# State-space input tables made from transposed factors on GpSimd, and the in-chunk kernel made from the output tables

## The chip, the cores and the metric

The kernel runs on one core of a Trainium2 chip. Its engines work side by side, each through its own list of instructions in order: TensorE (PE: matrix products and transposes), VectorE (DVE), ScalarE (ACT) and GpSimd (POOL). SyncE (SP) issues the transfers between DRAM and the on-chip memory, which 16 DMA engines carry out; its list too is worked off in order, and a transfer that has to wait for something holds up those behind it. The metric is the device time of one execution in microseconds (us), as the median of several runs.

## The reference, cut to what matters

The program is a two-layer encoder trunk on 1024 frames of 1024 channels. Its first layer has two branches, and the change concerns one of them, a diagonal complex state-space layer ("S5") over 64 groups of 16 channels with 64 states each, worked in chunks of 64 frames:

```python
lb_re = mag * jnp.cos(aim * dt);  lb_im = mag * jnp.sin(aim * dt)      # one pole per state
bb_re = coef_re[..., None] * bre - coef_im[..., None] * bim            # input matrix, group x state x 16
bb_im = coef_re[..., None] * bim + coef_im[..., None] * bre
...
bu_re = jnp.einsum('tbgh,gnh->tbgn', u_c, bb_re)                       # input of every state
bu_im = jnp.einsum('tbgh,gnh->tbgn', u_c, bb_im)
pr, pim, zr, zi = lax.associative_scan(_complex_affine_combine, (a_r, a_i, bu_re, bu_im), axis=0)
xr = zr + pr * s_re - pim * s_im                                       # states, with the carry
y = (jnp.einsum('tbgn,ghn->tbgh', xr, cre) - jnp.einsum('tbgn,ghn->tbgh', xi, cim) + dsk * u_c)
```

After it come a GELU and a gated linear unit. The second branch (retention) and the second layer (a convolution module) are untouched.

## The kernel before, in words

The state-space layer is not worked frame by frame. Frames are taken in strips of eight. Within a strip the output is a small triangular (Toeplitz) matrix applied to the eight frames, the in-chunk kernel; across strips the states are carried by a scan over 128 strips. The 64 groups are 32 pairs of groups, whose two times 64 states fill the 128 partitions, and the pairs go in eight blocks B of four.

Three pairs of tables are made per block, by `s5_tables` on GpSimd, each from small factors by `outer` (L785 to L792): for both the real and the imaginary part two products and one sum or difference, so six operations over 128x512 elements for a pair of tables and 18 for a block. All 18, of all blocks, are chained in the order in which they are written:

- Mr, Mi, the input tables: powers of the pole (`pr`, `pi`, step j = 0 to 7) times the input matrix (`bbr`, `bbi`), states on the partitions. The factors are read repeated (one along the 16 channels, the other along the eight steps).
- Tc, Ts, rotation factors for the scan.
- W3, the output tables: powers of the pole (steps 1 to 8) times the output matrix C (`cr`, `nci`).

`s5_states` (L830 to L897) then loads U, the block's input in strips, transposes M on TensorE into W2 (L837, eight transposes per block, each pair of banks copied by ScalarE at L839), multiplies W2 with U into v (L848), rotates and scans v on VectorE (L856 to L876) into the states S, and makes the in-chunk kernel `kp` from M and a block-diagonal copy of C (`cbr`, `cbni`, loaded; L882 and L883, eight products). The kernel is copied (Kg, L885), gets the direct term d on its first 16 columns (L886), is transposed on TensorE (kt, L888), copied (Kt, L890), stored to DRAM (L892, 64 KB), read back with overlapping rows as the Toeplitz matrix Wd (L895), and reordered into W1 (L897). `s5_out` (L912, L918) makes the output y of a block from W1, U, W3 and S, one block later.

All this runs beside a long sequence of ordinary products: `mm_u` (the input projection, eight column blocks `u_block`) and then `mm_g` (the gates, 16 column blocks, two to a state-space block). Each is a 1024-deep product in three passes (L276 to L278: high parts, low times high, high times low) on tiles of 128x512, 24 of them for half a column block. Below, "product n" counts these passes on TensorE from the start of the program. The weights for them, `wf_g`, are loaded by SP, cast by ScalarE (L267), and reduced to the low part by VectorE or GpSimd (L268). Other transfers in the same queue are the input sums (`xa`, `xt`) and weight sums (`a`, `ws`, `va`, `vs`) for later stages.

What order the instructions get on each engine is decided when the program is built, by a scheduler with a model of times; each engine then follows its list. Tables have buffers of their own: M and W2 one set, T and W3 two.

## Time and profile before

| | |
|---|---|
| runs | 1179.49, 1176.93, 1178.66 us; median 1178.66 |
| profiled execution: first to last instruction | 1173.9 us |
| median above that span | 4.8 us |
| granted clock of TensorE | 0.999 |
| TensorE busy | 1161.3 us, 99% |
| VectorE, ScalarE, GpSimd busy | 910.5, 545.1, 713.5 us |
| DMA, over the span | 270.66 MB, 231 GB/s |

The profile is of one execution; the span runs from its first to its last instruction, and the run's own time has the start and the end of the program besides. PE's busy time overlaps itself, as products are pipelined: one that is shown with 0.39 us starts about 0.23 us behind the one before it. A row of the timeline gives start, duration, engine, line, operation, tiles and count; a row of a group gives busy time and mean ns, and behind the second bar the idle time of the engine before it with what ended it; a row of the table of stretches gives the busy time of each engine with its instructions, the clock, the share of the DMA engines that was busy, and what they moved.

### The profile page before, as it was taken

To read this page: it belongs to the slowest core of one execution; us is meant where nothing else is said; L and a number is where in the kernel's file an instruction comes from. 1 tells how busy PE (TensorE), PEld (TensorE's weight loads), DVE (VectorE), ACT (ScalarE), POOL (GpSimd) and SP (SyncE) were. 2 spreads that over 40 slices of the span, in tenths; PEclk is the share of its full clock that TensorE was granted. 3 is DMA by queue.
4 is the path that set the end of the run, shared out by engine and by line. 5 is a ranking of instruction groups with operands and counts; after the bars stand their busy time and mean duration, and the time that the engine had idled before them with its cause. 6 is when DMAs were issued, how large, how long until landed. Compare 5 with 4: busy or idle time off the path is not lost.

```text
span 1173.9 us, 17492 instructions
## 1 busy us (share of the span) xinstructions
PE 1161.3 (99%) x6150; PEld 965.5 (82%) x6150; DVE 910.5 (78%) x1507; ACT 545.1 (46%) x821; POOL 713.5 (61%) x507
## 2 busy tenths in 40 slices
PE   9999999999999999999999999999999999999997
PEld 7888888888888888887788888888888888888887
DVE  7875789999717475689777888479999999999643
ACT  7212343332226642123645544367756678544662
POOL 2049999888843245664444034348894689977742
PEclk9999999999999999999999999999999999999999
DMA  9353378778789765765988468965448553357863
GB/s 344 109 178 109 134 270 312 272 269 282 273 307 325 268 228 192 251 190 180 362 313 304 160 220 268 309 232 188 161 158 306 216 182 132 134 176 243 281 247 138
DMA packets 131192, 270.66 MB, mean 231 GB/s; under 512 B 12832, under 2 KB 41760, under 8 KB 130976
## 3 DMA queue, kind: packets, MB, share of 16 engines
q1 hardware_dynamic: 129952, 265.35, 66.5%
q10 hardware_dynamic: 1152, 4.19, 0.9%
q8 instruction: 48, 0.79, 0.3%
q14 instruction: 40, 0.33, 0.1%
HBM read 193.54 MB, written 71.76 MB: 226 GB/s over the span
## 4 chain that ended last, share of the span: by engine, by line
PE 91%; DMA 4%; DVE 2%; SPq 1%; ACT 1%; POOL 1%; issue 1%; DVEq 0%; POOLq 0%; ACTq 0%
PE mm_g L277 8%; PE mm_g L278 8%; PE mm_g L276 7%; PE mm_w L278 4%; PE mm_w L277 4%; PE mm_w L276 4%; PE mm_a L278 2%; PE mm_b L277 2%; PE mm_a L276 2%; PE mm_b L278 2%; PE mm_a L277 2%; PE mm_b L276 2%; PE mm_u L278 2%; PE mm_oc L278 2%; PE mm_u L277 2%; PE mm_oc L277 2%
## 5 line engine op out<-in xcount | busy, mean ns | idle before, releaser
L1461 DVE SCALAR_TENSOR_TENSOR cv<-u,convw,cv 128x512 f32<-128x512 f32 x358 | 244.7, 750 | 5.0 <-ACT cv L1447 3.5
L1441 POOL TENSOR_TENSOR tp<-tp,tp 128x512 f32<-128x512 f32 x104 | 138.9, 1338 | 28.7 <-ACT tp L1440 23.4
L278 PE MATMUL mm_g<-xh,wl_g 128*128 128x512 f32 x256 | 100.8, 394 | 0.0
L277 PE MATMUL mm_g<-xl,wh_g 128*128 128x512 f32 x256 | 100.7, 394 | 0.0
L276 PE MATMUL mm_g<-xh,wh_g 128*128 128x512 f32 x256 | 100.5, 393 | 0.0
L1440 ACT ACTIVATE tp<-u,convw 128x512 f32<-128x512 f32 x104 | 69.6, 713 | 9.6 <-POOL tp L1441 9.4
L277 PEld LDWEIGHTS mm_g<-xl,wh_g 128*128 128x128 f32 x256 | 48.1, 188 | 11.2 <-issue 1.6
L278 PEld LDWEIGHTS mm_g<-xh,wl_g 128*128 128x128 f32 x256 | 48.0, 188 | 10.5
L276 PEld LDWEIGHTS mm_g<-xh,wh_g 128*128 128x128 f32 x256 | 48.1, 188 | 9.6
L278 PE MATMUL mm_oc<-zh,wl_woc 128*128 128x512 f32 (+1 forms) x152 | 54.5, 360 | 0.2 <-DMA wl_woc<-lo_woc 0.2
L276 PE MATMUL mm_oc<-zh,wh_woc 128*128 128x512 f32 (+1 forms) x152 | 54.3, 362 | 0.0
L277 PE MATMUL mm_oc<-zl,wh_woc 128*128 128x512 f32 (+1 forms) x152 | 54.0, 357 | 0.0
L276 PE MATMUL mm_glu<-yh,wh_glu 128*128 128x512 f32 x128 | 50.0, 392 | 1.3 <-ACT sg L1250 1.3
L277 PE MATMUL mm_u<-xl,wh_u 128*128 128x512 f32 x128 | 50.1, 391 | 1.0 <-DVE xl L390 0.9
L276 PE MATMUL mm_g<-h1h,wh_cg 128*128 128x512 f32 x128 | 50.3, 393 | 0.0
L276 PE MATMUL mm_a<-h1h,wh_ca 128*128 128x512 f32 x128 | 50.3, 393 | 0.0
L278 PE MATMUL mm_b<-h1h,wl_cb 128*128 128x512 f32 x128 | 50.3, 393 | 0.0
L232 ACT CAST lh<-lf 128x512 fp32r<-128x512 f32 x32 | 19.5, 618 | 65.9 <-DMA lf<-w_c 59.3
L278 PE MATMUL mm_a<-h1h,wl_ca 128*128 128x512 f32 x128 | 50.0, 391 | 0.0
L277 PE MATMUL mm_glu<-yl,wh_glu 128*128 128x512 f32 x128 | 50.0, 392 | 0.0
L278 PE MATMUL mm_g<-h1h,wl_cg 128*128 128x512 f32 x128 | 49.9, 390 | 0.0
L277 PE MATMUL mm_g<-h1l,wh_cg 128*128 128x512 f32 x128 | 49.9, 390 | 0.0
(811 smaller groups left out, 3637.3 us busy)
## 6 DMA issues: line engine op xcount, KB each, us to landing
wf_g<-w_ab SPq DMA_DIRECT2D x16, 512.0 KB, 5.4
a<-w_out SPq DMA_DIRECT2D x32, 256.0 KB, 4.4
ws<-a SPq DMA_DIRECT2D x32, 256.0 KB, 4.8
lf<-w_c SPq DMA_DIRECT2D x32, 256.0 KB, 5.3
wf_p<-ws SPq DMA_DIRECT2D x16, 512.0 KB, 4.1
wf_cb<-w_c SPq DMA_DIRECT2D x16, 512.0 KB, 4.9
wf_ca<-w_c SPq DMA_DIRECT2D x16, 512.0 KB, 4.7
wl_cb<-lo_cb SPq DMA_DIRECT2D x16, 512.0 KB, 3.4
```

The lines of the kernel that those rows point to most:

```text
L232: self.nc.scalar.copy(hi[:], f[:])
L276: nc.tensor.matmul(ps, wh[:, kb, :], xh, start=start, stop=False)
L277: nc.tensor.matmul(ps, wh[:, kb, :], xl, start=False, stop=False)
L278: self.last_mm = nc.tensor.matmul(ps, wl[:, kb, :], xh, start=False, stop=stop)
L1440: nc.scalar.mul(sk[:], u[:, k:k + HALF], cw[:, nb, k:k + 1])
L1441: gp.tensor_tensor(s0[:], s0[:], sk[:], op=ALU.add)
L1461: v.scalar_tensor_tensor(dst[:], *tap, accs_[i][:], op0=ALU.mult, op1=ALU.add)
```

## The change

The M tables and their transposes are gone. The transposed tables W2 are made directly:

- `s5_turned`, once, early in the sequence `mm_u`: TensorE transposes the powers of the pole (`pr`, `pi`, four transposes) and the input matrix (`bbr`, `bbi`, eight); ScalarE copies the results, and four stores put them into DRAM (`ptr`, `pti`, 128 KB each; `btr`, `bti`, 256 KB each).
- For this `bbr` and `bbi` are laid out with the channel ahead of the pair, and GpSimd writes them with a stride.
- Per block four loads of 256 KB read these back repeated: PTr, PTi have every step's row 16 times (once for each channel), BTr, BTi have the 16 channels' rows eight times. GpSimd multiplies them into W2 by `outer`, six operations over 128x512 elements with nothing repeated in the operands. The order in a block is now T, W2, W3. PT, BT and W2 have one buffer each, so the loads of a block wait for the W2 of the block before.
- W3 gets 16 columns more ahead of its 128, filled by ScalarE with C itself (two copies per block). The in-chunk kernel is the product of a block-diagonal copy of the input matrix (`bblk`, made once: two fills by GpSimd, four copies by ScalarE) and the first 128 of these columns. It comes out transposed as needed, so the transpose kt and its copy are gone; but its rows are then written to DRAM by eight stores per block, with runs of 16 elements (64 bytes) in DRAM, in place of one store with rows of 512 bytes.
- `cbr`, `cbi` (two loads of 512 KB at the start) and the negation of one of them are gone. The pool of the early tiles closes after the sixth `u_block` in place of the fourth.

```diff
+                if (nb, h) == (6, 0):
+                    with tc.issue_after(self.last_mm.ins):
+                        self.s5_turned(ev)
...
-        self.cbr, self.cbni = load("s5_cbr", (NP, 32)), load("s5_cbi", (NP, 32))
+        self.bblk = [sp.tile([P, NP, 32], F32, name=f"s5_bblk{c}") for c in "ri"]
+        for b in self.bblk:
+            nc.gpsimd.memset(b[:], 0.0)
...
-        tt(self.bbr[:], x1[0], x1[1], ALU.subtract, gp)
-        tt(self.bbi[:], x1[2], x1[3], ALU.add, gp)
+        tt(self.bbr[:].rearrange("p h q -> p q h"), x1[0], x1[1], ALU.subtract, gp)
+        tt(self.bbi[:].rearrange("p h q -> p q h"), x1[2], x1[3], ALU.add, gp)
+    def s5_turned(self, tp):
+        nc = self.nc
+        self.pt_d = [self.dram.tile([8, 32, P], F32, name=f"pt{c}") for c in "ri"]
+        self.bt_d = [self.dram.tile([16, 32, P], F32, name=f"bt{c}") for c in "ri"]
+        def turn(name, srcs, dsts):
+            ps = self.bank(f"turn_{name}")
+            for i, src in enumerate(srcs):
+                nc.tensor.transpose(ps[:, i * P:(i + 1) * P], src, self.ident[:])
+            t = tp.tile([P, 8, P], F32, name=f"turned_{name}", tag="xin", bufs=8)[:, :4, :]
+            nc.scalar.copy(t.rearrange("p i n -> p (i n)"), ps[:])
+            n = len(srcs) // len(dsts)
+            for i, dst in enumerate(dsts):
+                nc.sync.dma_start(dst.rearrange("(i p) n -> p i n", p=P), t[:, i * n:(i + 1) * n, :])
...
+        for blk, b in zip(self.bblk, (self.bbr, self.bbi)):
+            for g in range(2):
+                r = slice(64 * g, 64 * g + 64)
+                nc.scalar.copy(blk[r, :, 16 * g:16 * g + 16], b[r].rearrange("p h q -> p q h"))
...
-        Mr, Mi = self.big(f"Mr_{B}", "Mr", 1), self.big(f"Mi_{B}", "Mi", 1)
-        made = [self.outer(B, Mr[:], Mi[:], bj(self.bbr), bj(self.bbi), pj(self.pr), pj(self.pi), vm)]
...
+        made = [self.outer(B, Tc[:], Ts[:], ea(self.e2[0]), ea(self.e2[1]), eb(self.e1[0]), eb(self.e1[1]), vt)]
+        PT, BT = ([self.big(f"{n}{c}_{B}", n + c, 1) for c in "ri"] for n in ("PT", "BT"))
+        for t, d in zip(PT, self.pt_d):
+            nc.sync.dma_start(t[:], bass.AP(tensor=d.tensor, offset=d.offset + qs.start * P,
+                                            ap=[[32 * P, 8], [0, 16], [1, 4 * P]]))
+        for t, d in zip(BT, self.bt_d):
+            nc.sync.dma_start(t[:], bass.AP(tensor=d.tensor, offset=d.offset + qs.start * P,
+                                            ap=[[0, 8], [32 * P, 16], [1, 4 * P]]))
+        W2 = [self.big(f"W2{c}_{B}", f"W2{c}", 1) for c in "ri"]
+        made.append(self.outer(B, W2[0][:], W2[1][:], BT[0][:], BT[1][:], PT[0][:], PT[1][:], lambda ap: ap))
+        W3 = w.tile([P, 2, 4, 9 * 16], F32, name=f"W3_{B}", tag="W3", bufs=2)
+        for c, t in enumerate((self.cr, self.nci)):
+            nc.scalar.copy(W3[:, c, :, 0:16], t[:, qs, :])
+        made.append(self.outer(B, W3[:, 0, :, 16:], W3[:, 1, :, 16:], pj(self.pr), pj(self.pi), bj(self.cr),
+                               bj(self.nci), vm, ALU.add, ALU.subtract))
...
-        for nm, M in (("r", Mr), ("i", Mi)):
-            ps = self.bank(f"w2{nm}_{B}")
-            for q in range(4):
-                nc.tensor.transpose(ps[:, q * P:(q + 1) * P], M[:, q, :], self.ident[:])
-            t = self.big(f"W2{nm}_{B}", f"W2{nm}", 1)
-            nc.scalar.copy(t[:].rearrange("p q n -> p (q n)"), ps[:])
...
-        for q in range(4):
-            o = kp[q * 32:(q + 1) * 32, :P]
-            nc.tensor.matmul(o, self.cbr[:, q0 + q, :], Mr[:, q, :], start=True, stop=False)
-            nc.tensor.matmul(o, self.cbni[:, q0 + q, :], Mi[:, q, :], start=False, stop=True)
+        for c in range(2):
+            made += [nc.tensor.matmul(kp[q * 32:(q + 1) * 32, :P], self.bblk[c][:, q0 + q, :], W3[:, c, q, :P],
+                                      start=c == 0, stop=c == 1) for q in range(4)]
...
-        nc.tensor.transpose(kp[:, :P], Kg[:], self.ident[:])
-        Kt = w.tile([P, P], F32, name=f"Kt_{B}", tag="Kg", bufs=1)
-        nc.scalar.copy(Kt[:], kp[:, :P])
-        nc.sync.dma_start(self.k_d[B, 112:], Kt[:])
+        kd = self.k_d[B, 112:].rearrange("(j i) (g o) -> g i j o", j=8, g=8)
+        for g in range(8):
+            nc.sync.dma_start(kd[g], Kg[16 * g:16 * g + 16].rearrange("p (j o) -> p j o", j=8))
```

How the order of instructions moves is shown at three places. The first is TensorE at block 3, before (W2 was transposed earlier in the row; Mr and Mi are the tables, `s_s_cbr` is C):

```order
L276 MATMUL mm_g_0_2008<-xh_0_214,wh_g_1701 128x512
L848 MATMUL v_3_1942<-U_1926,W2r_1933 64x128 x8
L848 MATMUL v_3_1951<-U_1926,W2i_1940 64x128 x8
L882 MATMUL kp_1980<-Mr_1872,s_s_cbr 32x128
L883 MATMUL kp_1980<-Mi_1873,s_s_cbi 32x128
L882 MATMUL kp_1980<-Mr_1872,s_s_cbr 32x128
L883 MATMUL kp_1980<-Mi_1873,s_s_cbi 32x128
```

and the same block in the change:

```order
L278 MATMUL mm_g_1_1873<-xh_1_218,wl_g_1543 128x512
L881 MATMUL v_3_1967<-U_1965,W2r_1911 64x128 x8
L881 MATMUL v_3_1976<-U_1965,W2i_1912 64x128 x8
L914 MATMUL kp_2005<-W_3_1913,s_bblkr 32x128 x4
L914 MATMUL kp_2005<-W_3_1913,s_bblki 32x128 x4
L276 MATMUL mm_g_0_2036<-xh_0_134,wh_g_1730 128x512
```

Both islands are of one piece. kp reads W3 (`W_3`) in place of M. The island stood behind product 694 before and stands behind product 672 now (block 4: 790 and 775). In block 0 and in block 1 of the change, the two halves of v and the two halves of kp stand apart (v after products 400 and 405, kp after 421 and 432 in block 0), with gate products between them, where before they were one piece; y of block 0 stands behind product 528 (530 before).

The second place is TensorE at the transposes, before, ahead of gate product 385 (block 0; the same stands in every block):

```order
L278 MATMUL mm_u_1_1010<-xh_1_218,wl_u_860 128x512
L837 MATMUL w2r_1073<-ident,Mr_1037 128x128 x4
L837 MATMUL w2i_1080<-ident,Mi_1038 128x128 x4
L276 MATMUL mm_g_0_1153<-xh_0_134,wh_g_919 128x512
L277 MATMUL mm_g_0_1153<-xl_0_135,wh_g_919 128x512
```

and now, once, behind product 312 of the input projection:

```order
L278 MATMUL mm_u_0_916<-xh_0_214,wl_u_792 128x512
L796 MATMUL turn_p<-ident,s_pr 128x128 x2
L796 MATMUL turn_p<-ident,s_pi 128x128 x2
L796 MATMUL turn_br<-ident,s_bbr 128x128 x4
L796 MATMUL turn_bi<-ident,s_bbi 128x128 x4
L276 MATMUL mm_u_1_975<-xh_1_142,wh_u_791 128x512
```

The eight transposes of each block are gone, and twelve stand 72 products earlier than those of block 0 did.

The third place is SP's queue around the first loads of the factors:

```order
L454 DMA u_d<-ut_849 128x8x128
L265 DMA wf_g_1239<-w_ab 128x1024
L801 DMA ptr<-turned_p 128x2x128
L801 DMA pti<-turned_p 128x2x128
L801 DMA btr<-turned_br 128x4x128
L801 DMA bti<-turned_bi 128x4x128
L845 DMA PTr_1071<-ptr 128x1x512
L845 DMA PTi_1072<-pti 128x1x512
L848 DMA BTr_1073<-btr 128x1x512
L848 DMA BTi_1074<-bti 128x1x512
L872 DMA U_1113<-u_d 128x1024
```

Before, the U of block 0 followed the weight load directly. Now four stores and four loads stand between them. In the blocks behind it the eight stores of the kernel (L922) stand in the place of the one (L892), ahead of the reload Wd.

More of the change, by code (lines that the diff above doesn't have):

```diff
@@ L473, in layer0_front @@
         u_block(4)
+        for nb in (5, 6):
+            u_block(nb)
         early.close()
@@ L476, in layer0_front @@
         self.s5 = self.pool("s5w", 1, stack=st)
-        for nb in range(5, 8):
-            u_block(nb)
+        u_block(7)
         self.s5_tab, self.s5_back, self.s5_last = {}, {}, None
@@ L769, in s5_params @@
             tt(cfi[:], a1[:], rden[:], ALU.mult)
-        self.bbr, self.bbi = t((NP, 16), keep="s5_bbr"), t((NP, 16), keep="s5_bbi")
+        self.bbr, self.bbi = (tp.tile([P, 16, NP], F32, name=f"s5_bb{c}") for c in "ri")
         bc = lambda q: q[:].unsqueeze(2).broadcast_to([P, NP, 16])
@@ L778, in s5_params @@
         tt(x1[3], br[:], bc(cfi), ALU.mult, gp)
-        tt(self.bbr[:], x1[0], x1[1], ALU.subtract, gp)
-        tt(self.bbi[:], x1[2], x1[3], ALU.add, gp)
+        tt(self.bbr[:].rearrange("p h q -> p q h"), x1[0], x1[1], ALU.subtract, gp)
[13 more added lines that the diff above has]
+                nc.sync.dma_start(dst.rearrange("(i p) n -> p i n", p=P), t[:, i * n:(i + 1) * n, :])
+        fl = lambda t: t.rearrange("p a b -> p (a b)")
+        cols = lambda t, n: [fl(t)[:, i * P:(i + 1) * P] for i in range(n)]
+        rows = lambda d: d[:].rearrange("a b n -> (a b) n")
+        turn("p", cols(self.pr[:, 0:8, :], 2) + cols(self.pi[:, 0:8, :], 2), [rows(d) for d in self.pt_d])
+        for c, b in zip("ri", (self.bbr, self.bbi)):
+            turn(f"b{c}", cols(b[:], 4), [rows(self.bt_d["ri".index(c)])])
+        for blk, b in zip(self.bblk, (self.bbr, self.bbi)):
+            for g in range(2):
+                r = slice(64 * g, 64 * g + 64)
+                nc.scalar.copy(blk[r, :, 16 * g:16 * g + 16], b[r].rearrange("p h q -> p q h"))
     def big(self, name, tag, bufs):
@@ L799, in s5_tables @@
         qs = slice(4 * B, 4 * B + 4)
[L801 removed]
         vm = lambda ap: ap.rearrange("p q (j h) -> p q j h", j=8)
         bj = lambda t: t[:, qs, :].unsqueeze(2).broadcast_to([P, 4, 8, 16])
[L804 to L805 removed]
+        pj = lambda t: t[:, 1:9, qs].rearrange("p j q -> p q j").unsqueeze(3).broadcast_to([P, 4, 8, 16])
         Tc, Ts = self.big(f"Tc_{B}", "Tc", 2), self.big(f"Ts_{B}", "Ts", 2)
@@ L810, in s5_tables @@
         eb = lambda t: t[:, 0:16, qs].rearrange("p b q -> p q b").unsqueeze(2).broadcast_to([P, 4, 8, 16])
-        made.append(self.outer(B, Tc[:], Ts[:], ea(self.e2[0]), ea(self.e2[1]), eb(self.e1[0]), eb(self.e1[1]), vt))
-        W3 = w.tile([P, 2, 4, P], F32, name=f"W3_{B}", tag="W3", bufs=2)
-        made.append(self.outer(B, W3[:, 0], W3[:, 1], pj(self.pr, 1), pj(self.pi, 1), bj(self.cr), bj(self.nci), vm,
-                               ALU.add, ALU.subtract))
+        made = [self.outer(B, Tc[:], Ts[:], ea(self.e2[0]), ea(self.e2[1]), eb(self.e1[0]), eb(self.e1[1]), vt)]
[13 more added lines that the diff above has]
+                               bj(self.nci), vm, ALU.add, ALU.subtract))
         self.s5_last = self.chained(chain(*made), self.s5_last)
@@ L819, in s5_tables @@
             nc.scalar.mul(R8[:, q, :], self.m01[:], self.r8[:, 4 * B + q:4 * B + q + 1])
-        self.s5_tab[B] = Mr, Mi, W3, Tc, Ts, R8
+        self.s5_tab[B] = W2, W3, Tc, Ts, R8
     def s5_states(self, B):
@@ L876, in s5_states @@
         v.memset(S[:].rearrange("p c q m -> p (c q) m")[:, :, 0:1], 0.0)
-        kp = self.bank(f"kp_{B}")
-        for q in range(4):
-            o = kp[q * 32:(q + 1) * 32, :P]
-            nc.tensor.matmul(o, self.cbr[:, q0 + q, :], Mr[:, q, :], start=True, stop=False)
-            nc.tensor.matmul(o, self.cbni[:, q0 + q, :], Mi[:, q, :], start=False, stop=True)
+        kp, made = self.bank(f"kp_{B}"), []
+        for c in range(2):
+            made += [nc.tensor.matmul(kp[q * 32:(q + 1) * 32, :P], self.bblk[c][:, q0 + q, :], W3[:, c, q, :P],
+                                      start=c == 0, stop=c == 1) for q in range(4)]
+        self.chained(made)
         Kg = w.tile([P, P], F32, name=f"Kg_{B}", tag="Kg", bufs=1)
@@ L917, in products @@
                         r = slice(64 * g2, 64 * g2 + 64)
-                        yield nc.tensor.matmul(ps[g2][:, cols(q)], W3[r, c, q, :], S[r, c, q, :],
+                        yield nc.tensor.matmul(ps[g2][:, cols(q)], W3[r, c, q, 16:], S[r, c, q, :],
                                                start=False, stop=q == 3 and c == 1)
@@ L1739, in layout @@
     A["s5_cr"], A["s5_ci"] = c(inp["s5_c_re"][0]), c(inp["s5_c_im"][0])
-    for k in ("r", "i"):
-        cc = A["s5_c" + k].reshape(2, 64, 32, 16)
-        z = np.zeros((2, 64, 32, 2, 16), f)
-        for g in range(2):
-            z[g, :, :, g, :] = cc[g]
-        A["s5_cb" + k] = z.reshape(P, 32, 32)
     dd = np.zeros((8, 8, 16, 16), f)
```

7 lines of the change are left out of this document (1 added, 6 removed).

## The prediction

> **What bounds the kernel now.** I read the first and second parts of the page, then the table of stretches for the time in which the tables are made (60 to 333 us) and the stage behind it, then the waits of PE, then the order of single instructions at the places of the change.
>
> ```profile
> span 1173.9 us, 17492 instructions
> PE 1161.3 (99%) x6150; PEld 965.5 (82%) x6150; DVE 910.5 (78%) x1507; ACT 545.1 (46%) x821; POOL 713.5 (61%) x507
> ```
>
> PE is busy for 1161.3 of 1173.9 us. So whatever leaves PE shortens the end, and whatever makes PE wait lengthens it, one for one, while work on other engines counts only where PE waits for it.
>
> ```profile
> core 0: us, PE busy (x) PEld busy (x) DVE busy (x) ACT busy (x) POOL busy (x), PEclk, DMA share, GB/s
> 12.00:30.00 18.00, 17.13 (x75) 14.19 (x76) 17.65 (x24) 13.76 (x19) 3.27 (x2) 1.00 0.98 374
> ...
> 97.00:126.60 29.60, 29.60 (x173) 24.28 (x173) 16.64 (x21) 8.98 (x16) 28.58 (x23) 1.00 0.29 92
> ...
> 156.10:185.60 29.50, 29.50 (x204) 24.69 (x202) 25.98 (x31) 10.54 (x19) 26.95 (x19) 1.00 0.75 265
> 185.60:215.10 29.50, 29.50 (x204) 24.69 (x202) 28.16 (x32) 9.90 (x19) 27.33 (x20) 1.00 0.86 301
> ...
> 274.10:303.60 29.50, 29.50 (x204) 24.68 (x203) 27.36 (x30) 8.03 (x14) 25.74 (x19) 1.00 0.80 276
> ...
> 333.00:396.00 63.00, 63.00 (x309) 52.53 (x308) 32.21 (x36) 33.06 (x39) 19.95 (x14) 1.00 0.97 323
> ```
>
> Each row from 97 to 333 us (a part of them is shown) is one block of the state space beside its 96 gate products of 128x512: 29.5 us in which PE never stops, at clock 1.00. POOL (GpSimd) is the next engine: 25.7 to 28.6 us of 29.5. The DMA engines have room early (share 0.29) and little from the fourth block on (0.75 to 0.86, then 0.97). In these stretches PE waits for nothing. The change moves work off PE and onto POOL and the DMA engines, which are the two with the least to spare.
>
> **What leaves PE.** The eight transposes of M into W2, block 0, and one transpose of the in-chunk kernel:
>
> ```profile
> 100.90 0.60 PE L837 MATMUL w2r<-ident,Mr 128*128 128x128 f32 x4
> 101.34 0.60 PE L837 MATMUL w2i<-ident,Mi 128*128 128x128 f32 x4
> 101.69 0.48 PE L276 MATMUL mm_g<-xh,wh_g 128*128 128x512 f32 x1
> 102.01 0.40 PE L277 MATMUL mm_g<-xl,wh_g 128*128 128x512 f32 x1
> ...
> 115.65 0.39 PE L277 MATMUL mm_g<-xl,wh_g 128*128 128x512 f32 x1
> 115.88 0.27 PE L888 MATMUL kt<-ident,Kg 128*128 128x128 f32 x1
> 115.90 0.48 PE L278 MATMUL mm_g<-xh,wl_g 128*128 128x512 f32 x1
> 116.22 0.40 PE L276 MATMUL mm_g<-xh,wh_g 128*128 128x512 f32 x1
> ...
> 188.18 0.39 PE L278 MATMUL mm_g<-xh,wl_g 128*128 128x512 f32 x1
> 191.13 0.39 PE L276 MATMUL mm_g<-xh,wh_g 128*128 128x512 f32 x1
> ```
>
> Durations overlap, so starts are what counts. One product of 128x512 takes 0.227 us from start to start (188.18 to 191.13 with 13 of them, no other work between). From 100.90 to 101.69 the eight transposes take 0.79 us, and the first product behind them 0.32 (to 102.01) in place of 0.227: 0.88 us. The single one takes 116.22 − 115.88 = 0.34 less 0.227: 0.12 us. Eight blocks: 8 × 0.88 + 8 × 0.12 = **−8.0 us**.
>
> **What comes to PE.** Twelve transposes, once, of the same shape: 0.79/8 = 0.099 each and the passage 0.09, **+1.3 us**. The kernel kp keeps eight products per block of the same size, with other operands. But the order changes in blocks 0 and 1:
>
> ```profile
> 106.58 0.39 PE L276 MATMUL mm_g<-xh,wh_g 128*128 128x512 f32 x1
> 106.90 1.09 PE L848 MATMUL v<-U,W2r 128*64 128x128 f32 x16
> 107.82 1.04 PE L848 MATMUL v<-U,W2i 128*64 128x128 f32 x16
> ...
> 109.39 0.50 PE L277 MATMUL mm_g<-xl,wh_g 128*128 128x512 f32 x1
> 109.73 0.39 PE L278 MATMUL mm_g<-xh,wl_g 128*128 128x512 f32 x1
> ```
>
> The fence shows an island of v and kp, which stands in one piece; eight kp products follow the v rows and end it at 109.39. Going in costs 0.32 − 0.227 and coming out 0.34 − 0.227, 0.2 us together. In blocks 0 and 1 of the change four pieces stand at four places, three islands more each: six by 0.2, about **+1.0 us** (bounds 0.6 and 1.4, by 0.1 and 0.23 each). Without any wait the sum is −8.0 + 1.3 + 1.0 = **−5.7 us**, and a block in the steady part takes 28.5 us in place of 29.5.
>
> **What comes to POOL.** The groups of the removed M tables, all blocks and the first block of the next:
>
> ```profile
> L790 POOL TENSOR_TENSOR o<-s_bbi,s_pi 128x512 f32<-128x512 f32 x8 | 13.8, 1720 | 0.1
> L792 POOL TENSOR_TENSOR Mr<-Mr,o 128x512 f32<-128x512 f32 x8 | 11.3, 1413 | 0.6
> L792 POOL TENSOR_TENSOR Mi<-Mi,o 128x512 f32<-128x512 f32 x8 | 11.0, 1370 | 0.6
> L790 POOL TENSOR_TENSOR o<-s_bbi,s_pr 128x512 f32<-128x512 f32 x8 | 10.0, 1249 | 0.0
> L791 POOL TENSOR_TENSOR Mr<-s_bbr,s_pr 128x512 f32<-128x512 f32 x8 | 8.9, 1114 | 15.3 <-PE kp L883 15.3
> L791 POOL TENSOR_TENSOR Mi<-s_bbr,s_pi 128x512 f32<-128x512 f32 x8 | 8.9, 1110 | 0.0
> ```
>
> M costs 63.9/8 = 8.0 us a block. W2 is six products of contiguous operands; the like of them are the L792 rows, 1.29 us when single (s_bbr below) and 1.39 in the mean: 7.7 to 8.4. So POOL's load hardly changes, about +0.2 us a block. The 15.3 us in which Mr waited for kp is its whole slack over seven blocks, 2.2 us a block. What changes is the start and what each PE step needs. Before, M is first in a block and both v and kp need M alone. Now the order is T, W2, W3; v needs W2 (two thirds through) and kp needs W3, the last: a full block of POOL, not a third.
>
> **When the first W2 can start.** Rows of the path: two of POOL in order of time, the cast and a weight load of SP's queue likewise; a group of ACT; and three kinds of transfers (size, median us from issue to landing).
>
> ```profile
> 80.39 1.29 POOL L607 TENSOR_TENSOR s_bbr<-s5bb 128x512 f32<-128x512 f32 x1
> 81.64 1.29 POOL L607 TENSOR_TENSOR s_bbi<-s5bb 128x512 f32<-128x512 f32 x1
> ...
> 84.08 1.03 ACT L267 CAST wh_g<-wf_g 128x1024 fp32r<-128x1024 f32 x1
> ...
> 93.50 0.33 SPq L265 DMA_DIRECT2D wf_g<-w_ab  x1
> ...
> L839 ACT COPY W2r<-w2r 128x512 f32<-128x512 f32 x8 | 4.6, 579 | 0.0
> ...
> a<-w_out SPq DMA_DIRECT2D x32, 256.0 KB, 4.4
> ...
> Wd<-k_d SPq DMA_DIRECT2D x8, 512.0 KB, 5.1
> ...
> k_d<-Kt SPq DMA_DIRECT2D x8, 64.0 KB, 1.5
> ```
>
> The factor bbi is done at 82.9; its write is now strided, which no row of this size on POOL shows, so between 82.9 and 84.6 (twice as long for both). ACT then does four block copies (at half the partitions, 0.58 each at most), the cast of 1.03 that stands between, and three copies of 0.58: at most 5.1 us, ending at about 88. SP issues the four stores behind the weight load wf_g (0.33 to 0.36 each); the last is issued at 88 to 90.5 and lands after 1.5 (the 64 KB row) to 4.4 us (the 256 KB row): 90 to 93.5. Only then can the loads read it back; another 4.4 us: the start S of W2 lies at **95.3** (93.6 to 97.9). POOL makes T meanwhile, about 10 us of the 26, and sits idle then.
>
> From S, W3 of block 3 is W2 and W3 of block 0 (7.7 to 8.4, and about the 8.0 of M, which is made of the same kinds: 15.7 to 16.4) and three whole blocks of 26.4 (POOL's column in the stretches, 25.7 to 27.3 behind the first, with the 0.2 more): S + 95.2 = 190.5. PE in the order of the change has kp of block 3 ahead of gate product 672, v of the same block before had 694:
>
> ```profile
> 191.45 1.09 PE L848 MATMUL v<-U,W2r 128*64 128x128 f32 x16
> ```
>
> 22 products less are 5.0 us: 186.4; less four W2 islands (3.5) and three kernel transposes (0.4), plus the 1.3 and 1.0 from above and the v of block 3 itself (1.9): PE arrives at **186.8 to 187.8**. It waits 190.5 − 187.3 = 3.2 us, between 0.5 (S at 93.6, later arrival) and 6 (S at 97.9). Blocks 1 and 2 come within 1 us of waiting by the same count, so part of the stall may fall there; the sum is the largest lateness, not each added. From block 4 on kp stands 103 products behind the last, 23.3 + 6.8 us of islands against POOL's 26.4: PE has 3 us to spare and no further wait. What queues behind kp while PE waits is all of PE's gate products, so the stall is given back in full. I take 3.2 to 4, by the middle of S: **+3.7**.
>
> **The rest.** SP gets four loads and seven more stores of the kernel a block (11 × 0.33 = 3.6 us of issue in 28.5). W1 is read a block later, 96 products or more behind kp (22 to 33 us), and takes some 12 us (eight issues 2.6, landing 1.5 to 4.4, reload 5.1, and a copy of 1024 elements at the 1.03 of the cast): hidden by 10 us. Two fills by POOL stand at the very start, where POOL sat idle (3.27 us of 18 in the first row), and two loads of 512 KB leave that stretch, where the DMA share is 0.98: between 0 and −1 us, as PE is at 17.13 of 18; I take 0. The twelve transposes stand ahead of product 312, the first W2 before stood at 384 (100.90): 72 products earlier is 84.5 us, so they wait for bbi by 0.1 us at most. Sum: −5.7 + 3.7 = −2.0 us; I take −1.7, as blocks 1 and 2 are so near. The profiled span of 1173.9 lies 4.8 us below the median of 1178.66; I take the 4.8 to stay. 1172.2 + 4.8 = **1177.0 us**.
>
> **Rivals.** (1) *POOL keeps up.* With S at 93.6 and 1.29 us per product (W2 7.7), W3 of block 3 is there at 186.9, and the lateness goes to zero and the whole saving stays: 1178.7 − 5.7 = **1173.0**. For it: POOL is held up by PE for 15.3 us before, so it has a lead it does not use. Against: the first read-back comes 12 us after bbi, where before M began at once.
>
> (2) *The loads crowd the DMA engines: slower.* Each block loads 1.05 MB more. At 374 GB/s for a share of 0.98 an engine moves 23.9 GB/s, so on 16 engines this is 2.75 us of a block's 28.5. But the loads' source has eight repeats as its outermost dimension; if that decides how many engines share one, each of eight engines gets 5.5 us. In the fourth block these would need 0.86 × 29.5 + 5.5 = 30.9 us of 28.5 available, and 0.80 × 29.5 + 5.5 = 29.1 in each of the four later ones: 2.4 + 4 × 0.6 = 4.8 us behind. Behind them stands a stage at 0.97, which can take up 1.9 us of its 63. A load twice as long makes S later by 2.5 too. Together −1.7 + (4.8 − 1.9) + 2.5 = +3.7: **1182.5** (1180 to 1188). It decides as soon as eight engines carry the loads. Against: transfers are issued ahead, and PE does not wait at 0.97.
> The Trainium skill ("DMA: Bandwidth & Descriptors", "Why a DMA increments its semaphore by 16 and not by 1" and "Rules for kernel authors") says that the slowest dimension larger than one of each access pattern sets the number of engines, and that a leading broadcast of c copies confines a DMA to c of them. By that rule rival 2's condition holds; no transfer of the profile before shows it, so it stays a chance.
>
> (3) *The kernel's path is late.* The store of the kernel is written in runs of 64 bytes, 1024 packets in place of 128. If each costs what one of 512 bytes does, a store takes 8 × 1.5 = 12 us, and W1 is there 21 us after kp (2.6 + 12 + 5.1 + 1.0), just inside the 22 of block 0. At twice that cost it is 33 us, and y of block 0 comes 9 us late (paid once, as later blocks have more between): about 1186. Nothing in the profile shows such a packet.
>
> **Chances.** Forecast 0.43, rival (1) 0.28, rival (2) 0.23, rival (3) 0.06. The forecast's own range is 1174.5 to 1179.5 (S and the arrival). The range to hold 8 in 10 takes in most of (1) and half of (2) and goes from 1172.5 to 1184. A measurement of this kernel can tell about 0.2% (2.4 us) from no change, so faster means under 1176.3: (1) and somewhat over a quarter of the forecast, 0.40; slower over 1181.0: four fifths of (2) and all of (3), 0.24; the rest, 0.36, within.
>
> **What would show it.** No L837 or L888 on PE, and the stretch of a later block 1 us shorter. A wait of PE at kp for POOL's W3 in block 3 (or 1 and 2) of 3 to 4 us and nothing in later blocks; S, the first W2 product, at 95. Under (1) no such row. Under (2) the median landing of the PT and BT loads is far above 4.4 us, and PE waits for weight transfers after 330 us. Under (3) y waits for W1. The prediction is wrong if PE waits at v, or if the products of W2 take over 1.6 us each.

## The result

The changed kernel takes 1209.24 us (median of 4 runs, 1208.18 to 1212.16), the kernel before beside it 1178.97 (4 runs). The ratio is 1.0268, 95% interval 1.0252 to 1.0284: 30 us slower, where 1177.0 was forecast and the range ended at 1184.0. The profiled execution has a span of 1206.4 us, 32.5 more than before.

First the page of the changed kernel (span, busy time, and the chain that ended last by engine):

```profile
span 1206.4 us, 17526 instructions
PE 1168.4 (97%) x6090; PEld 969.5 (80%) x6090; DVE 905.3 (75%) x1506; ACT 544.0 (45%) x820; POOL 717.6 (59%) x509
PE 78%; DMA 12%; POOL 3%; DVE 3%; SPq 1%; issue 1%; ACT 1%; DVEq 0%; POOLq 0%; ACTq 0%
```

PE has 60 instructions fewer and is busy 7 us longer, and transfers stand for 12% of the last chain in place of 4%. The waits of PE over the whole program (us in total, times, longest) say where it stood still:

```profile
PE v L881 <- DMA U<-u_d: 21.1, 5, 8.5
PE v L881 <- POOL W2r L824: 3.7, 1, 3.7
PE mm_glu L276 <- ACT sg L1280: 1.6, 1, 1.6
...
PE v L881 <- POOL W2i L824: 1.0, 2, 0.8
```

The longest of the kernel before was this one:

```profile
PE mm_glu L276 <- ACT sg L1250: 1.3, 1, 1.3
```

All that is new is at v, the product of W2 with U: 25.8 us, of which 21.1 are waits for U, a load that the change does not touch. There is no wait at kp, where the forecast had one. The long ones in the order of time (start, duration; in brackets the wait ahead):

```profile
109.90 1.98 PE L881 MATMUL v<-U,W2r 128*64 128x128 f32 x16 [3.69 <-POOL W2r L824]
174.02 1.94 PE L881 MATMUL v<-U,W2r 128*64 128x128 f32 x16 [3.30 <-DMA U<-u_d]
202.62 1.98 PE L881 MATMUL v<-U,W2r 128*64 128x128 f32 x16 [4.08 <-DMA U<-u_d]
243.88 1.97 PE L881 MATMUL v<-U,W2r 128*64 128x128 f32 x16 [8.55 <-DMA U<-u_d]
306.97 1.77 PE L881 MATMUL v<-U,W2r 128*64 128x128 f32 x16 [4.97 <-DMA U<-u_d]
```

Each of the five has a second price. The v products behind such a wait take 1.77 to 1.98 us for 16 (1.09 before): TensorE runs at half clock. The table of stretches shows it, for two of the blocks, and for short stretches at and behind a wait (columns as in the table before: length, busy time of PE, PEld, DVE, ACT and POOL, granted clock of PE, DMA share, GB/s):

```profile
97.00:126.60 29.60, 25.65 (x134) 19.67 (x133) 14.02 (x18) 8.50 (x14) 20.18 (x16) 0.88 0.76 240
...
215.10:244.60 29.50, 20.95 (x128) 17.61 (x128) 22.06 (x22) 7.88 (x15) 27.04 (x19) 0.90 0.88 274
...
109.20:116.10 6.90, 5.93 (x35) 4.59 (x37) 1.71 (x1) 3.63 (x5) 6.82 (x6) 0.51 0.91 323
239.00:249.20 10.20, 5.32 (x50) 4.50 (x51) 6.71 (x8) 4.38 (x7) 6.71 (x6) 0.50 0.99 368
249.30:270.00 20.70, 20.70 (x124) 17.53 (x123) 13.97 (x22) 6.55 (x13) 12.11 (x10) 1.00 0.84 284
```

After the wait of 8.55 us the clock is 0.50 for the 5.3 us in which PE works again, and 1.00 from 249.3 on. Stretches of 0.1 and 0.2 us at the edges show that the half rate at the five waits holds for 6.8, 3.4, 6.8, 10.3 and 3.4 us. Some 24 of these 31 us are work (the rest falls into the waits themselves), and at half rate they cost 12 us. The mean over the span is near that: granted 0.987 (0.999 before) is 0.013 × 1206 = 15.7 us of clock lost, less 1.2 before, less 3.4 within the waits, about 11. The account then closes: −5.7 (the removed products, as forecast) + 25.4 (waits of PE, 31.5 in all less 6.1 before) + 12 (half clock) = 31.7 of the measured 32.5 us.

The Trainium skill ("TensorE: Matmul & The Clock Gate", "Part 1: The HAM clock gate") says that an idle window of about 3.4 us brings the half rate and that a busy one of the same length ends it. The lengths of the half rate agree: one, two or three times 3.4 us. The lengths of the waits agree only in part. In all the runs below each wait of 3.6 us or more was followed by the half rate, but so were some shorter ones (3.30 here, 2.96 in the run with one store, 2.29 in the last run but one), while one of 3.50 us in the run with one store was not.

Where does lateness come from? The factors come back late (POOL in order of time, SP's queue, and two transfers of the last chain with start and duration):

```profile
90.36 1.29 POOL L824 TENSOR_TENSOR Ts<-Ts,o 128x512 f32<-128x512 f32 x1
106.03 1.26 POOL L822 TENSOR_TENSOR o<-BTi,PTi 128x512 f32<-128x512 f32 x1 [14.37 <-DMA BTi<-bti]
```

```profile
91.07 0.62 SPq L801 DMA_DIRECT2D bti<-turned_bi  x1
93.80 0.74 SPq L845 DMA_DIRECT2D PTr<-ptr  x1
...
96.27 0.58 SPq L848 DMA_DIRECT2D BTi<-bti  x1
...
129.44 4.50 SPq L922 DMA_DIRECT2D k_d<-Kg  x8
135.06 0.38 SPq L925 DMA_DIRECT2D Wd<-k_d  x1
```

```profile
91.07 4.56 DMA bti<-turned_bi
...
96.27 9.62 DMA BTi<-bti
```

The last store lands at 95.6, and only then are the loads of BT issued; the last of them goes out at 96.3 and lands at 105.9. So S is 106.0, not 95.3. While the loads are alone (the next transfer, U of block 0, is issued at 96.9), less than half of the 16 engines are busy:

```profile
95.50:98.00 2.50, 2.50 (x13) 2.07 (x12) 0.81 (x1) 0.00 (x0) 0.00 (x0) 1.00 0.42 158
```

The Trainium skill ("DMA: Bandwidth & Descriptors", "Rules for kernel authors") has an outermost dimension of fewer than 16, such as a leading broadcast, confine a DMA to at most as many engines, eight here; a share of 0.42 agrees. The 9.6 us of the last load are not the price of the eight engines alone, though: from 100 to 104 us, with U and other transfers issued behind it, the share is 1.01. The last chain in the stretch from 225 to 250 us shows what happens to an ordinary transfer behind a block's loads (start, duration):

```profile
228.14 9.52 DMA a<-w_out
237.72 7.10 DMA ws<-a
```

These 256 KB load in 4.4 us and store in 4.8 us in the median of before. U itself, from its issue in SP's queue to the v that waits for it:

```profile
167.97 0.38 SPq L872 DMA_DIRECT2D U<-u_d  x1
...
236.50 0.32 SPq L872 DMA_DIRECT2D U<-u_d  x1
...
296.19 1.19 SPq L872 DMA_DIRECT2D U<-u_d  x1
```

With v at 174.02, 243.88 and 306.97 that is 6.1, 7.4 and 10.8 us. Before, all eight landings of U, and the issue of U of block 3, were these:

```profile
DMA to landing us min/median/max: 3.4/4.6/7.7
176.82 1.59 SPq L830 DMA_DIRECT2D U<-u_d  x1
```

That U, which took the 7.7 us, was issued 14.6 us ahead of its v at 191.45; those of blocks 2 to 7 had 14.6 to 18.4 us and mostly landed in 3.4 to 4.0. So the landing is longer in the change, but above all the issue is late. In block 4 of the change TensorE stood at v from 235.3 on (243.88 less 8.55), and U went out at 236.5, after that.

### The profile page after: what moved, and what is told of

Read it like the earlier page. It is cut to its first block, busy times and chain, and to the rows that moved or that the text cites. A ratio compares the mean times of both kernels' runs of the same rounds, so it can differ in the third digit from the quotient of the medians.

```text
span 1206.4 us, 17526 instructions
## 1 busy us (share of the span) xinstructions
PE 1168.4 (97%) x6090; PEld 969.5 (80%) x6090; DVE 905.3 (75%) x1506; ACT 544.0 (45%) x820; POOL 717.6 (59%) x509
## 4 chain that ended last, share of the span: by engine, by line
PE 78%; DMA 12%; POOL 3%; DVE 3%; SPq 1%; issue 1%; ACT 1%; DVEq 0%; POOLq 0%; ACTq 0%
PE mm_w L278 4%; PE mm_w L276 4%; PE mm_w L277 4%; PE mm_g L276 4%; PE mm_g L277 4%; PE mm_g L278 4%; PE mm_a L278 2%; PE mm_b L278 2%; PE mm_a L276 2%; PE mm_b L276 2%; PE mm_b L277 2%; PE mm_a L277 2%; PE mm_oc L278 2%; PE mm_oc L277 2%; PE mm_oc L276 2%; PE mm_v L1092 2%
## 5 line engine op out<-in xcount | busy, mean ns | idle before, releaser
L277 PEld LDWEIGHTS mm_g<-xl,wh_g 128*128 128x128 f32 x256 | 48.6, 190 | 10.8 <-issue 1.5
L277 PE MATMUL mm_b<-h1l,wh_cb 128*128 128x512 f32 x128 | 49.8, 389 | 0.0
```

Source lines behind the costliest of these rows:

```text
L277: nc.tensor.matmul(ps, wh[:, kb, :], xl, start=False, stop=False)
```

## The experiments

A "step" is a single edit of the changed kernel, unless said otherwise; every run stands beside runs of the kernel before on the same chip (1177 to 1179 us). The theories were: A, the loads sit on eight engines; B, SP's queue is held up by the number of issues; C, the bytes are too many; D (formed later), U has too little time between its buffer and its use.

### Loads on 16 engines

```diff
-ap=[[32 * P, 8], [0, 16], [1, 4 * P]]      # PT
+ap=[[0, 16], [32 * P, 8], [1, 4 * P]]
-ap=[[0, 8], [32 * P, 16], [1, 4 * P]]      # BT
+ap=[[32 * P, 16], [0, 8], [1, 4 * P]]
```

> The change with the source dimensions of the PT and BT loads the other way round: 16 outermost, eight within. Same bytes, same packets, same order of every instruction; the rows of PT and BT land on other partitions than U's, so the numbers of this branch are wrong, while all work is done. Theory A (the loads sit on eight of the 16 engines, and what is queued behind them on these, U above all, lands late): S, the first W2 product, falls from 106.0 to about 100 us, the waits of v for U from 21.1 to under 5 us, and the time by 20 to 27 us, to 1182 to 1189. Theory B (SP's queue is held up by the number of issues, so U is issued late): S falls by 4 and U's waits stay over 12 us; the time falls by 4 to 8 us. Theory C (8.4 MB more are too much traffic, however spread): under 4 us.

Measured 1198.35 us, ratio to before 1.0175 [1.0151, 1.0199]: 11 us off the change. The order of all instructions is the same, so this is the price of the eight engines. But S falls only to 104.65 and U is still late:

```profile
PE v L881 <- DMA U<-u_d: 15.2, 4, 4.6
PE v L881 <- POOL W2i L824: 2.2, 1, 2.2
PE v L881 <- POOL W2r L824: 1.9, 1, 1.9
```

```profile
97.00:99.00 2.00, 2.00 (x10) 1.67 (x9) 1.12 (x1) 0.00 (x0) 0.00 (x0) 1.00 0.61 164
```

With 16 engines open to them the loads move 164 GB/s at a share of 0.61 (158 at 0.42 on eight): hardly faster, though more engines are busy. (U of block 0 is issued at 97.3; in the 1 us before it the figures are 162 and 0.58.) Theory A is a part, not the whole. The same with U, the kernel's store and its reload put in the same order of rows (edit in short):

```diff
-U[:] <- u_d[B].rearrange("j h g m -> (j h) g m")
+U[:] <- bass.AP(u_d[B], ap=[[8 * P, 16], [P * P, 8], [1, 8 * P]])
-self.k_d = dt("k_d", [8, 112 + P, P])
+self.k_d = dt("k_d", [8, 16, 15 * P])      # channel ahead of step; stores and zeros likewise
-Wd[:] <- ap=[[P, P], [16 * P, 8], [1, P]]
+Wd[:] <- ap=[[15 * P, 16], [P, 8], [1, 8 * P]]
```

> The loads on 16 as outermost dimension, with U, the store of the kernel and its reload put in the same order of rows (channel ahead of step), so the numbers are right; the reload Wd then has runs of 4 KB in place of 512 bytes. Theory A: as the spread loads alone, 1180 to 1189, the reload shorter. Theory B: 1200 to 1206. Theory C: over 1204.

1198.23 us, 1.0175 [1.0149, 1.0201], the same; the longer runs of Wd gained nothing.

### One store in place of eight

```diff
-for g in range(8):
-    nc.sync.dma_start(kd[g], Kg[16 * g:16 * g + 16].rearrange("p (j o) -> p j o", j=8))
+nc.sync.dma_start(self.k_d[B, 112:], Kg[:])
```

> The change with one store of the kernel per block (64 KB in rows of 512 bytes) in place of eight; the kernel's elements then stand in the wrong order in DRAM, so the output is wrong, while the bytes, the reload and the products stay. 56 issues fewer in SP's queue. Theory A: the waits for U shrink by a quarter at most, the time by 0 to 6 us. Theory B: U is issued 3 to 5 us earlier in every block from the third on and its waits fall from 21 to under 8 us; with the clock that goes with each the time falls by 15 to 22 us. Theory C: under 3 us.

1194.63 us, 1.0144 [1.0119, 1.0169]: 15 us off. The order on TensorE changes with it: the island of block 2 stands behind product 576 in place of 601, that of block 4 behind 768 in place of 775. Both are earlier, which by itself leaves U less room, not more. The waits for U fall to 6.6, and waits at kp of 6.1 us come up, both in block 2, for GpSimd's W3 as the forecast had it:

```profile
PE v L881 <- DMA U<-u_d: 6.6, 3, 3.5
PE kp L914 <- POOL W L824: 6.1, 2, 3.3
```

With the same eight stores issued from ScalarE's queue:

```diff
-            nc.sync.dma_start(kd[g], ...)
+            nc.scalar.dma_start(kd[g], ...)
```

> The change with the eight stores of the kernel issued from ScalarE's queue in place of SP's: 64 issues fewer in SP's queue, and nothing in SP's queue waits for the kernel before a store; the numbers are right. Theory B: near the single store, 1190 to 1196, as SP is relieved by the same issues; under 1190 if waiting for the kernel, too, held the queue. Theory A: 1203 to 1209.

1197.68 us, 1.016 [1.0132, 1.0188]. The bytes and the number of transfers are those of the change, and the order on TensorE is that of the run before it, so what is saved, 11.6 us, is SP's queue. The stores in runs of 64 bytes are not slow as such: the reload in the fence above, which waits for them, is issued 1.1 us behind the end of their issue.

### No reload, and a quarter of it

```diff
-PT, BT = ([self.big(f"{n}{c}_{B}", n + c, 1) ...])
+if B == 0:
+    self.ptbt = [[self.big(f"{n}{c}_{B}", n + c, 1) ...]]
+PT, BT = self.ptbt                           # loads for B == 0 only
```

> The change with PT and BT loaded for block 0 alone; later blocks multiply block 0's factors, so their numbers are wrong. 28 loads and 7.3 MB fewer, S as before. Theories A and C: the waits for U in blocks 2 to 6 go to under 3 us and with them the half clock behind them; what is left is block 0 (3.7 us of wait and 3 of clock): 1182 to 1186. Theory B: 28 of 84 added issues go, so waits for U stay at 10 us or more: 1192 to 1202.

1184.02 us, 1.0056 [1.0035, 1.0077]: 25 us off. Waits for U are gone (0.6 us); what is left is GpSimd's lateness from block 0 on (the 3.8 us in block 2, whose island stands where it does in the change):

```profile
PE v L883 <- POOL W L824: 3.8, 1, 3.8
PE v L883 <- POOL W2r L824: 2.3, 1, 2.3
PE v L883 <- POOL W2i L824: 2.2, 1, 2.2
PE kp L916 <- POOL W L824: 0.8, 1, 0.8
PE v L883 <- DMA U<-u_d: 0.6, 1, 0.6
```

9.7 us of waits, and half clock after two of them (granted 0.996): 6.7 slower than before although 5.7 are saved, so 12.4 us is what the late start costs, eight stores included. Then the loads were left in place, but with one of four pairs from block 1 on:

```diff
-nc.sync.dma_start(t[:], bass.AP(..., [1, 4 * P]]))
+nc.sync.dma_start(t[:, :nq], bass.AP(..., [1, nq * P]]))     # nq = 4 in block 0, else 1
```

> The change with PT and BT of blocks 1 to 7 loaded for the first of four pairs only (64 KB in place of 256, runs of 512 bytes; the rest are block 0's factors, so the numbers are wrong). As many issues in SP's queue, a quarter of the bytes, a third of the engines' time. If the loads cost by what they move: near the run without reloads, 1184 to 1190. If by their issues and their place in the queue: 1200 to 1209.

1188.51 us, 1.0094 [1.0078, 1.0109]. All issues are there and 21 of the 25 us are off: the reload costs by what it moves.

### Where U is issued, and how many buffers it has

```diff
-nc.sync.dma_start(U[:], ...)
+nc.scalar.dma_start(U[:], ...)
```

> The change with U issued from ScalarE's queue in place of SP's; loads on eight engines, eight stores and all bytes as they were. Theory B (U is late because SP issues it late, behind stores and loads that wait): U is issued right behind y of the block two before, 10 us or more earlier, and its waits fall from 21 to under 4 us; what remains is POOL's lateness of 4 to 8 us, and the time is 1184 to 1190. Theory A (U lands late because its share on the eight engines stands behind the loads): U still takes 6 to 10 us to land; waits of 10 us or more stay, and the time is over 1195.

1208.34 us, 1.0248 [1.023, 1.0265]: nothing gained. In blocks 2 and 3 the waits for U are gone, in their place are waits for POOL, and in blocks 4 to 6 U is late as before:

```profile
PE v L881 <- DMA U<-u_d: 16.7, 3, 7.8
PE kp L914 <- POOL W L824: 4.8, 3, 2.8
```

So theory D was formed: from block 3 on, y frees U's buffer only 48 to 55 products ahead of v (68 before). A third buffer takes that away:

```diff
-U = w.tile([P, 8, P], F32, name=f"U_{B}", tag="U", bufs=2)
+U = w.tile([P, 8, P], F32, name=f"U_{B}", tag="U", bufs=3)
-self.big(f"m{i}_{B}", "tmpV", 4)             # and d: space for it
+self.big(f"m{i}_{B}", "tmpV", 2)
```

> The change with three buffers of U in place of two (the space comes from two in place of four scratch tiles of VectorE's products). U of a block then does not wait for y of the block two before, and stands a block earlier in SP's queue; loads on eight engines, stores and bytes as they were. Theory D (U's load has only the 48 to 55 products between y, which frees its buffer, and v, which reads it, 11 us for the queue and the landing): the 21 us of waits for U go to under 2 us and the half clock of four of five stops with them; POOL's lateness of about 10 us, hidden behind them so far, shows: 1186 to 1192. Theories A and B (queue and engines are overloaded as such): other loads become late in U's place, the weights above all; the time stays over 1198.

1205.57 us, 1.0233 [1.0212, 1.0254]. No wait for U is left and the time is the same:

```profile
PE v L881 <- ACT yb L952: 11.4, 3, 5.8
PE kp L914 <- POOL W L824: 6.3, 2, 3.9
PE v L881 <- DVE S L907: 3.1, 1, 3.1
```

Theory D falls. The lateness goes on to what has the least room next: v now waits for y to leave its bank, behind ScalarE's copy of y. Ahead of that copy in ScalarE's order stands the one of Wd, which waited 6.9 and 15.1 us for its reload at the two longest of these places.

### Block 0

GpSimd's order in block 0 as T, W3, W2:

```diff
+if B == 0:
+    made[1:] = made[:0:-1]
```

> The change with block 0 alone in the order T, W3, W2 on GpSimd (six operations of 8 us that need no load move into the 14 us in which GpSimd waits for the first loads). v of block 0 moves 30 products later on TensorE. If the late first read-back is what makes the waits of blocks 0 to 2, these go (v for W2 of block 0: 3.7 + 0.3 us and 3 of half clock) while the waits for U from block 3 on stay at 17 us or more: the time falls by 5 to 9 us, to 1200 to 1204. If the lateness of U hangs on it too (everything of block 0 is earlier), the waits for U fall by half and the time goes to 1190.

1207.66 us, 1.0253 [1.0227, 1.028]. The wait for W2 of block 0 is gone and the time is not: U is late by 21.3 us, and v of block 3 waits 9.3 us for GpSimd, the longest wait of this run. Block 0 in the way of before:

```diff
+if B == 0:
+    M = ...; made.insert(0, self.outer(B, M[0][:], M[1][:], ...))   # M on GpSimd, eight transposes in s5_states
```

> The change with block 0 alone made in the way of before: M on GpSimd right behind the input matrix, eight transposes on TensorE; blocks 1 to 7 as in the change. GpSimd no longer waits for the first read-back (14 us). POOL's lateness goes, so no wait of v or kp for it; the waits for U stay, since they begin at block 2: at least 15 us of the 21. Theory D: 1196 to 1203. If the late start is what makes U late (U waits for y, y for S and W3, these for POOL): under 1190.

1206.78 us, 1.0241 [1.0207, 1.0275]; waits for U 23.1 us, and 4.9 us for ScalarE's copy of the transposed table in block 0. Neither moves the end while the reload makes U late.

### Put together

> All together, numbers right: loads on 16 engines (U, store and reload in the same row order), U and the kernel's stores issued from ScalarE, block 0 in the order T, W3, W2. By the sum of the parts no wait of v for U over 1 us is left and none over 2 us for POOL, so no half clock: the removed transposes remain, 1173 to 1178. If the rows read at once by many engines are still slow and POOL waits for them: 1180 to 1186.

The edits are those above: the loads on 16 with rows reordered, U and the stores issued from ScalarE, and W3 first in block 0. 1186.4 us, 1.0063 [1.0046, 1.008]; the best of those that leave nothing out, and still slower than before:

```profile
PE kp L918 <- POOL W L824: 5.3, 2, 2.9
PE v L885 <- ACT W L855: 3.2, 1, 3.2
PE v L885 <- DMA U<-u_d: 2.5, 1, 2.5
```

With block 0 in the way of before and three buffers of U in place of U's queue and the order in block 0, and the same with the stores in SP's queue:

> Numbers right: block 0 in the way of before, three buffers of U, loads on 16 engines, the kernel's stores issued from ScalarE. No wait of v or kp is left if theory D and the late start are the whole of it: the removed transposes less block 0's and less the split islands, 1173.5 to 1176.5 beside a before of 1178.5. If SP's queue or the rows read by many engines at once still make loads late: 1180 to 1190.

> As the run before it with the eight stores of the kernel left in SP's queue. Theory D: within 2 us of it. Theory B (the number of issues in SP's queue counts by itself): 5 to 15 us slower than it.

1191.27 us (1.0112 [1.0091, 1.0133]) and 1194.92 (1.0146 [1.012, 1.0172]). In the first the waits are small and many; they stand at ScalarE's copies of W2 in block 0 (3.8) and of y (5.6 in four). Spread loads and one store together, without more:

> Both single steps at once: the loads with 16 outermost and one store of the kernel per block in place of eight (numbers wrong in both respects). The steps took 11 and 15 us off alone. If they are two causes that add: 1182 to 1186. If both relieve one and the same shortage (the 16 engines and SP's queue together), less than the sum: 1188 to 1194.

1187.45 us, 1.0082 [1.0066, 1.0099]: 22 us off where the single steps took 11 and 15. They relieve, in part, the same shortage.

### The loads alone, in the kernel before

Four loads per block were added to the kernel before, into tiles that nothing reads, first on eight, then on 16 engines:

```diff
+for k in range(4):
+    X = self.big(f"X{k}_{B}", f"X{k % 2}", 1)
+    nc.sync.dma_start(X[:], bass.AP(u_d ..., ap=...))      # 128x512; eight outermost, or 16
```

> The kernel before, with four loads of 256 KB added in every block into tiles that nothing reads: same places in the program and the same shapes as PT and BT, eight repeats or eight steps outermost, from a table of the kernel. The order on TensorE is that of the kernel before, and v and y stand where they stood. If the traffic of the reload by itself makes U and the others late: slower by 8 to 20 us, waits of v for U. If it needs the change's own order as well (U with 11 us from buffer to use in place of 15, 64 stores): slower by under 4 us.

> As the run before it with 16 as the outermost dimension of the added loads. If eight engines are the point, within 2 us of the kernel before while the other is slower; if bytes or issues, the two are alike within 3 us.

1211.45 us (1.0294 [1.0275, 1.0312]) and 1202.47 (1.0212 [1.0197, 1.0227]). Eight engines against 16 is 9 us here too. But the total says little: as nothing held the loads, SP ran through most of them at once, each waiting for the one before it in its tile, and the kernel's store came behind twelve of them (SP's queue of the second):

```profile
118.55 24.27 SPq L819 DMA_DIRECT2D X<-u_d  x12
142.85 0.59 SPq L896 DMA_DIRECT2D k_d<-Kt  x1
```

So they were repeated with tiles that GpSimd reads in its chain, which gives them the places of PT and BT:

```diff
+X = [w.tile([P, 480], F32, name=f"X{k}_{B}", tag=f"X{k}", bufs=1) for k in range(4)]
+for k, t in enumerate(X):
+    nc.sync.dma_start(t[:], bass.AP(u_d ..., ap=[[32 * P, 8], [0, 16], [1, 480]]))   # k > 1: [0, 8], [32 * P, 16]
+def seen():
+    for x in X:
+        yield gp.tensor_copy(t[:, 0, 0:1], x[:, 479:480])
+made.append(seen())                          # between T and W3
```

> The kernel before with four added loads per block of 240 KB, eight repeats or eight steps outermost like PT and BT, each tile read by one small copy on GpSimd in the chain of tables between T and W3, so that the loads of a block go out when the block before has passed there (in the two runs before, nothing held them, and they went out all at once). One buffer of R8 in place of two, two scratch tiles of VectorE in place of four, for space. TensorE's order is that of the kernel before. If the reload's traffic alone is the cause: slower by 12 us or more, with waits for U. If it needs the change's order (U with 11 us from buffer to use, kp behind W3, the late start): slower by 0 to 5 us.

1198.36 us, 1.0172 [1.0144, 1.02]: 21 us slower than before, with every product on TensorE in the order of before, no product added, and U never late. Here the largest wait is this one (timeline of PE and of DVE):

```profile
212.52 0.48 PE L898 MATMUL kt<-ident,Kg 128*128 128x128 f32 x1 [6.14 <-DVE Kg L896]
...
205.17 1.27 DVE L250 TENSOR_TENSOR a<-a,a 128x512 f32<-128x512 f32 x1 [8.84 <-DMA a<-w_out]
```

```profile
185.60:215.10 29.50, 21.06 (x126) 17.35 (x126) 20.15 (x23) 5.53 (x10) 21.52 (x17) 0.85 0.86 296
```

```profile
195.31 9.78 DMA a<-w_out
```

The transpose kt waits for Kg, which stands on VectorE behind sums of weights for a later stage, as it did before; these waited 8.84 us for their load. That load went out right behind three of the added ones and took 9.78 us (median before 4.4). To make room, this run also gives R8 (factors of the scan) one buffer in place of two and VectorE two scratch tiles in place of four; no run has these two steps alone. The waits of v for ScalarE's copy of W2 (3.4 us, two) can't be put down to them: ahead of both copies ScalarE had waited for other work, 6.3 us for a gate and 13.5 us for the reload of Wd. The same with the kernel's store in eight pieces:

```diff
-nc.sync.dma_start(self.k_d[B, 112:], Kt[:])
+for g in range(8):
+    nc.sync.dma_start(self.k_d[B, 112 + 16 * g:128 + 16 * g], Kt[16 * g:16 * g + 16])
```

> The run before it with the kernel's store in eight pieces of 8 KB as well: all of the change's transfers, all of the order and the tables of before. If queue and traffic together are the cause whatever the order: slower by 20 us or more, near the change and its 5.7 us. If the order is needed: slower by under 8 us.

1200.85 us, 1.0187 [1.0156, 1.0219]. The stores alone add 2.5 us here, within the uncertainty of the two; in the change, whose queue has more in it, they were worth 12 to 15.

So the loss of 36 us (30 measured and 5.7 saved) comes to this: 21 to 25 us for the traffic of the reload (21 in the kernel before, 25 by leaving it out of the change), 9 to 11 of them for the eight engines, and the remaining 12 for the late start and SP's eight stores together, which no run parts. The edits do not add up singly, as they share the queue.

What stays open: why loads on 16 engines move only 164 GB/s at a share of 0.61, where 374 GB/s at 0.98 was seen. In them many engines read the same few rows; a reload of as many bytes from rows that differ wasn't tried, so that this is the cause is argued only.

## Why the prediction was wrong

**What leaves PE and what comes to it: right.** −8.0 + 1.3 + 1.0 = −5.7 us closes the account of waits and clock to within 1 us. It is also seen directly where waits are few: without the reload, v of blocks 5 and 7 start 57.61 us apart with one wait of 0.65 between, 28.5 us a block as forecast. (Six islands by 0.2 are 1.2 and not 1.0.)

**POOL's load and the need for W3: right in kind, hidden.** Five of the six W2 operations of block 0 took 1.26 to 1.27 us, one 2.14. A wait for W3 came up as soon as U was no longer late: 3.8 us at v of block 2 without the reload, and 6.1 and 6.3 us at kp of block 2 with one store and with three buffers of U, where that island stands 25 products earlier. The forecast was 3.7, in block 3 or in 1 and 2. That 3.8 lies so near is luck, as S was 10.7 us later than the sum had it.

**When the first W2 can start: the term that was mis-sized first.** S was 95.3 with a bound of 97.9; it is 106.0. About half of the difference is the stores: the last was issued at 91.1 (forecast 88 to 90.5) and landed 4.6 us later, at 95.6 in place of 90 to 93.5. The other half is "another 4.4 us": the four loads were issued one behind the other from 93.8 to 96.9, and the last landed 9.6 us behind its issue. The row used for it was that of loads of 256 KB from 128 different rows; the text itself held that eight engines might carry these, and used the faster price. The bounds were too narrow even by their own terms: 88 + 1.5 and 90.5 + 4.4 are 89.5 and 94.9, and two writes of twice 1.29 us from 80.39 on end at 85.5, not 84.6 (they took 1.30 and 1.31 us).

**"The rest" was the step that failed.** SP's issues were priced at 0.33 us, as those of quiet times; eight stores took 4.50 us in block 0 (0.56 each), with 0.43 us for one in the median of all 64 and up to 1.67. And the loads were hidden by the argument that PE never waits at a DMA share of 0.97. That stage is one in which nothing else was added. What mattered was the room that each single transfer has between issue and use. U had 14.6 to 18.4 us before (blocks 2 to 7) and took 3.4 to 7.7 of it; in the change it was issued much later, in block 4 after TensorE had come to v, and the three loads shown took 6 to 11.

**Rival 2 named the mechanism and lost it in the price.** Its condition held (share 0.42 in the stretch where the loads are alone), its sign too. It was priced at +3.7 us by an average: work of eight engines over the time of a block, a backlog of 4.8 us by the end. By measurement the reload costs 21 to 25 us. An average share under 1 does not say that no transfer is late: loads come in bursts, a transfer behind a burst takes twice its time (9.52 and 9.78 us for a load with a median of 4.4), the engine that needs it works in order, and what stands behind it there waits too. None of this is in a backlog at the end.

**No price was put on the clock.** Five waits of 3.3 us and more cost 25 us as time and 12 as half clock behind them. The profile before has no wait of PE over 1.3 us in its body, so no row of it could show this.

**Rivals 1 and 3** did not come about: POOL could not keep up with a first load at 106, and the 64-byte stores were done within 1.1 to 1.5 us of the end of their issue in the six blocks where the reload follows them. (Rival 3's 33 us would have been 11 late, not 9. And the page before did count packets of under 512 bytes, 12832 of them.)

## What to carry to other kernels

A load that is "hidden" is to be checked not by the share of the DMA engines but transfer by transfer: for the ones that stand behind it in the queue, the time from issue to use before, and what is left if they take twice as long. On a kernel whose TensorE never waits, 1.05 MB more per block of 28 us bought 1 us of products and cost 3 us, and moving the loads, the queue or the buffers took off part of the loss at best and left the rest at another wait. And where TensorE is the bound, a wait has a second price: in the change the half clock behind the long ones cost about half as much again as the waits.

## What was not expected of the hardware

Four loads that read few rows many times moved 158 GB/s on eight engines and 164 on 16. Eight stores of 8 KB in runs of 64 bytes landed within 1.1 to 1.5 us of the end of their issue, so their price is mostly the issue (0.43 us in the median, up to 1.67, where the prediction had 0.33), not the runs. The half clock behind a wait lasted one, two or three times 3.4 us, and whether a wait of 2.3 to 3.5 us brought it did not follow from its length.
